# One late store of a cross-covariance attention kernel, cut into seven parts on two queues in place of four on one

## The chip, the cores and the metric

The kernel runs on one core of a Trainium2 chip. A core has five engines with instruction streams of their own: TensorE (PE), VectorE (DVE), ScalarE (ACT), GpSimd (POOL) and SyncE (SP). SP computes nothing; here it issues transfers. A transfer (DMA) moves data between the main memory (HBM) and the on-chip memory (SBUF, 128 partitions), and it is carried out by sixteen DMA engines that all queues share. A transfer is split over several of these engines; each moves its part in packets and closes it with a write of 4 bytes to a semaphore. The transfer has landed when all of those have come.

The metric is the time of one execution on the device in microseconds (us). The time before is the median of three runs, 128.60 us (128.47 to 128.75). The profile is of one more execution, of 128.35 us. Times within it are counted from its first instruction.

## The reference

Q, K and V are 8 x 12 x 512 x 64 (batch, heads, sequence, dim), in fp32. For each of the 96 heads:

```python
Q_norm = Q / (np.linalg.norm(Q, axis=-2, keepdims=True) + 1e-10)
K_norm = K / (np.linalg.norm(K, axis=-2, keepdims=True) + 1e-10)
attn = np.einsum('bhnd,bhne->bhde', Q_norm, K_norm)      # 64 x 64, over the sequence
attn = np.exp(attn - np.max(attn, axis=-1, keepdims=True))
attn = attn / (np.sum(attn, axis=-1, keepdims=True) + 1e-10)
out = np.einsum('bhnd,bhde->bhne', V, attn)
```

The inputs are 37.75 MB and the output 12.58 MB.

## The kernel before

**Tiling.** The heads are taken four at a time (a unit, 24 of them) and the units in pairs: twelve steps `s` = 0 to 11. A step loads its Q and K, casts them to bf16 (line 212), and forms the products Q'Q, Q'K and K'K of each head in one 128 x 128 Gram matrix on TensorE (line 232). The diagonal gives the norms, a quarter of the matrix the logits. Norms, exponentials and row sums follow on DVE, ACT and POOL (lines 239 to 290). V is loaded, cast (lines 168 and 170), transposed on TensorE (line 301) and multiplied with the attention matrix (line 318). The results are copied from PSUM into output tiles `so` (line 166 on ACT, line 168 on DVE) and stored.

**Stores.** A step has two output tiles, `so[s, 0]` and `so[s, 1]`, each filled by two copies; a tile is 128 partitions x 2 halves x 2 KB (512 KB), so that a store is 256 rows of 2 KB. Store 0 or 1 of step `s` goes out as one transfer (line 206), but for the store `FEW = (S - 3, 1)`, which is (9, 1), the sixth from the end: it leaves in four transfers, partitions 0 to 91, 92 to 99 and 100 to 127 of the first half (line 203) and all 128 of the second half (line 204). Two steps, and so four whole stores, follow it. There are thirteen `so` buffers.

**Order.** The program order of each engine is written by a planner (class `Order`): every piece of work has engines that may do it with a cost, pieces that it waits for, and a rank; pieces are placed one by one at the time at which the planner expects them to begin, and are then emitted in that order. Transfers are pieces of an engine called "DMA", and all but two early loads are issued on SP's queue, in the planner's order. `store` is called at its place in this order, whichever queue it issues on. The store (9, 1) is placed after the last piece of work of GpSimd, the scaling of K for step 11 (line 262).

**Waits.** A store waits for the two copies into its tile. Besides, SP's transfers take turns on eight semaphores, so that SP issues one only when the eighth before it has landed. The last thing that the program does is to wait until every transfer has landed, and then close.

Of the kernel before, what the change touches and what calls it, by code (L numbers as in the profile page):

```python
# [102 lines left out]
def kernel(  # L103
# [7 lines left out]
    nc = tc.nc  # L111
# [50 lines left out]
    qk32, v32, vb, qkb, gram, scr, kq, n2, r8, kqs, rq, lg, ex, ab, vps, vt, po, so = ({} for _ in range(18))  # L162
# [35 lines left out]
    def store(s, i):  # L198
        o = Of[s // 2, s % 2, i].rearrange("p r (j d) -> p r j d", d=D)
        if (s, i) == FEW:  # L200

            for a, b in ((0, 92), (92, 100), (100, 128)):
                nc.sync.dma_start(out=o[a:b, 0], in_=so[s, i][a:b, 0])
            nc.sync.dma_start(out=o[:, 1], in_=so[s, i][:, 1])
            return
        nc.sync.dma_start(out=o, in_=so[s, i])

# [139 lines left out]
    for i in range(NB["ab"]):  # L347
        a = const.tile([128, HU, 2 * D], BF16, name=f"ab{i}")
# [42 lines left out]
    for u in range(U):  # L391
        s, r = divmod(u, 2)
# [21 lines left out]
    for w in range(W):  # L414
        both = 2 * w >= BOTH
        for r in range(2):
            halves = (0, 1) if (w, r) == (W - 1, 1) else (None,)
            n = 2 * w + r - NB["v"]
# [22 lines left out]
    for s in range(S):  # L441
        for x in range(4):
            i, k = divmod(x, 2)
            n = 4 * s + x - 2
            wait = [("oc", n // 4, n % 4)] if n >= 0 else []
            order = [("ou", s, x - 1) if x else back("ou", s, 1, 3)]
            piece(("ou", s, x), {"PE": 0.5}, [("vc", s // 2, *t) for t in turns(s // 2) if t[0] // 2 == k] + [("nm", s)] + wait, order, R["ou"] + 0.01 * s, outs, s, x)
            n = 2 * s + i - NB["so"]
            free = [("st", n // 2, n % 2)] if k == 0 and n >= 0 else []
            order = [("oc", s, x - 1) if x else back("oc", s, 1, 3)]  # L450
            piece(("oc", s, x), {"ACT": 0.6, "DVE": (0.68, BIAS["oc"])} if s >= BOTH else {"ACT": 0.6}, [("ou", s, x)] + free, order, R["oc"] + 0.01 * s, ocopy, s, x)
        for i in range(2):
            order = [("st", s, 0) if i else back("st", s, 1, 1)]
            piece(("st", s, i), {"DMA": X}, [("oc", s, 2 * i), ("oc", s, 2 * i + 1)], order, v_at(2 * s + i) + ST_LAG, store, s, i)
# [43 lines left out]
```

## Time and profile before

| | |
|---|---|
| median of three runs | 128.60 us (128.47 to 128.75) |
| the profiled execution | 128.35 us |
| its span, first to last instruction | 126.5 us |
| busy: PE, DVE, ACT, POOL | 78.9, 90.7, 72.5, 37.4 us |
| moved over the span | 50.64 MB, 400 GB/s |
| SP's queue q1, share of the sixteen DMA engines' time | 96.5% |
| store (9, 1): its four issues on SP begin | 110.7 to 114.5 us |
| last compute instruction (ACT's copy into the last tile) ends | 115.6 us |

How to read it: a row of the second part of the page cuts the span into 40 slices of 3.16 us; a digit is the busy share in tenths, and GB/s is what all DMA engines moved together. A timeline line is start, length, engine, line, operation, output and input, and a count where like instructions are merged; an engine's name with a q (SPq) is its sequencer, which issues transfers. A table of windows gives for each stretch its length, each engine's busy time with the number of instructions, the clock granted to TensorE, the busy share of the DMA engines and GB/s. Packets of one engine overlap by some nanoseconds in the records, which is why that share can read 1.05 when all sixteen are full.

### The profile page before, as it was taken

Reading aid. Unit: us, or ns where it says so; the run is one execution under the profiler, and the core shown is the slowest. Engines: PE = TensorE matmul, PEld = TensorE weight load, DVE = VectorE, ACT = ScalarE, POOL = GpSimd, SP = SyncE. Lnnn points to the kernel's source line nnn. Section 1 sums busy time; section 2 is a strip of 40 time slices with the busy share of each in tenths; the row PEclk is TensorE's granted clock in tenths of the full one; section 3 lists DMA queues with packets and bytes.
Section 4 is the critical chain, followed back from the end, with each engine's and each line's share of the span. In section 5 each row is a group of like instructions: output and inputs, shape, how many; then the busy total and the mean of one; then the engine's idle time right before and its main releaser. Section 6 shows DMA issues by size and latency. Waiting matters only on the chain.

```text
span 126.5 us, 4885 instructions
## 1 busy us (share of the span) xinstructions
PE 78.9 (62%) x2128; PEld 64.2 (51%) x2128; DVE 90.7 (72%) x141; ACT 72.5 (57%) x220; POOL 37.4 (30%) x40
## 2 busy tenths in 40 slices
PE   0065393895964679958583999596676858473000
PEld 0054382784843568747372788484464746352000
DVE  3344749839899499899976798999999799740000
ACT  4000441539789077695883688694758969974000
POOL 4006307300745913043064303133363270300000
PEclk9999999999599555899998559959999999855555
DMA  3999999999999999999999999999999999999993
GB/s 129 408 434 411 427 413 421 413 434 408 430 417 418 409 422 417 398 414 425 422 417 412 418 419 421 416 423 423 401 415 411 402 401 407 400 407 408 405 382 149
DMA packets 15359, 50.64 MB, mean 400 GB/s; under 512 B 1130, under 2 KB 1130, under 8 KB 13930
## 3 DMA queue, kind: packets, MB, share of 16 engines
q1 hardware_dynamic: 15050, 49.29, 96.5%
q10 hardware_dynamic: 288, 1.05, 2.1%
q8 instruction: 16, 0.26, 0.7%
q14 instruction: 5, 0.04, 0.1%
HBM read 37.75 MB, written 12.58 MB: 398 GB/s over the span
## 4 chain that ended last, share of the span: by engine, by line
DVE 34%; DMA 21%; PE 19%; ACT 10%; issue 5%; POOL 2%; SPq 0%; DVEq 0%; ACTq 0%; POOLq 0%
DMA qk<-in_Q_dram 21%; DVE qkb L212 12%; PE gram L232 12%; DVE scr L239 7%; DVE ab L290 5%; ACT so L166 4%; PE po L318 3%; DVE vb L168 3%; ACT ex L281 3%; PE vps L301 3%; DVE n L251 3%; DVE vt L168 2%; ACT vt L166 2%; DVE so L168 1%; POOL kqs L262 1%
## 5 line engine op out<-in xcount | busy, mean ns | idle before, releaser
L232 PE MATMUL gram<-qkb 32*128 32x128 bf16 (+1 forms) x1504 | 36.9, 262 | 20.3 <-DVE qkb L212 7.1
L232 PEld LDWEIGHTS <-qkb 32*128 32x128 bf16 (+1 forms) x1504 | 31.0, 117 | 24.8 <-DVE qkb L212 8.9
L212 DVE CAST qkb<-qk 128x1024 bf16<-128x1024 f32 x48 | 35.3, 758 | 8.4 <-DMA qk<-in_Q_dram 6.8
L170 POOL TENSOR_SCALAR vb<-v 128x1024 bf16<-128x1024 f32 x19 | 22.0, 1169 | 43.9 <-DMA v<-in_V_dram 39.6
L166 ACT COPY so<-po 128x512 f32<-128x512 f32 x45 | 24.8, 593 | 6.6 <-PE po L318 6.5
L166 ACT COPY vt<-vps 128x1024 bf16<-128x1024 bf16 (+1 forms) x18 | 17.8, 987 | 16.5 <-PE vps L301 16.4
L318 PE MATMUL po<-ab,vt 128*64 128x128 bf16 x384 | 20.8, 252 | 5.1 <-ACT so L166 1.7
L301 PE MATMUL vps<-identb,vb 128*128 128x128 bf16 x192 | 18.4, 247 | 6.5 <-POOL vb L170 4.3
L262 POOL TENSOR_TENSOR kqs<-kq,r 64x512 f32<-64x512 f32 x12 | 14.1, 1171 | 26.7 <-ACT r L258 14.0
L239 DVE SCALAR_TENSOR_TENSOR scr<-gram,eye 64x512 f32<-64x512 f32 x24 | 16.5, 687 | 6.0 <-PE gram L232 5.8
L318 PEld LDWEIGHTS <-vt 128*64 128x64 bf16 x384 | 15.2, 127 | 9.4 <-issue 4.8
L301 PEld LDWEIGHTS <-vb 128*128 128x128 bf16 x192 | 13.5, 110 | 10.2 <-POOL vb L170 5.5
L281 ACT ACTIVATE ex<-lg,rq 128x64 f32<-128x64 f32 x48 | 14.5, 322 | 2.5 <-PE lg L275 2.3
L166 ACT COPY kq<-gram 64x512 f32<-64x512 f32 x12 | 7.0, 581 | 13.5 <-DVE scr L239 13.3
L290 DVE TENSOR_TENSOR ab<-ex,rinv 64x256 bf16<-64x256 f32 x24 | 13.4, 556 | 0.6
L281 ACT ACTIVATION_READ_ACCUMULATOR ex<-lg,rq 128x1 f32 x48 | 10.2, 213 | 0.0
L275 PE MATMUL lg<-eye,kqs 64*128 64x64 f32 x48 | 6.4, 258 | 4.3 <-POOL kqs L262 2.6
L251 DVE TENSOR_REDUCE n<-scr 128x8 f32<-128x512 f32 x12 | 8.1, 679 | 0.1
L168 DVE COPY vt<-vps 128x1024 bf16<-128x1024 bf16 (+1 forms) x8 | 7.9, 1020 | 0.1
L168 DVE CAST vb<-v 128x1024 bf16<-128x1024 f32 x5 | 7.0, 1399 | 1.3 <-DMA v<-in_V_dram 1.3
L275 PEld LDWEIGHTS lg<-eye,kqs 64*128 64x128 f32 x48 | 4.5, 156 | 6.1 <-POOL kqs L262 3.3
L287 DVE RECIPROCAL rinv<-esum 128x4 f32<-128x4 f32 x12 | 2.1, 172 | 3.4 <-ACT ex L281 3.2
(17 smaller groups left out, 16.0 us busy)
## 6 DMA issues: line engine op xcount, KB each, us to landing
out_dram<-so SPq DMA_DIRECT2D x23, 512.0 KB, 10.2
v<-in_V_dram SPq DMA_DIRECT2D x11, 1024.0 KB, 17.1
qk<-in_Q_dram SPq DMA_DIRECT2D x8, 1024.0 KB, 17.1
qk<-in_K_dram SPq DMA_DIRECT2D x8, 1024.0 KB, 17.9
qk<-in_Q_dram SPq DMA_DIRECT2D x8, 512.0 KB, 12.2
qk<-in_K_dram SPq DMA_DIRECT2D x6, 512.0 KB, 12.5
qk<-in_K_dram ACTq DMA_DIRECT2D x2, 512.0 KB
v<-in_V_dram SPq DMA_DIRECT2D x2, 512.0 KB
```

The lines of the kernel that those rows point to most:

```text
L166: nc.scalar.copy(o, i)
L168: nc.vector.tensor_copy(o, i)
L170: nc.gpsimd.tensor_scalar(out=o, in0=i, scalar1=1.0, scalar2=0.0, op0=ALU.mult, op1=ALU.add)
L212: nc.vector.tensor_copy(qkb[u][:, :, x * D:(x + 1) * D], qk32[s][:, x, r])
L232: nc.tensor.matmul(gram[s][:, h, r, 0], x, x, start=(t == 0), stop=(t == (T if u < WIDE else J) - 1))
L239: nc.vector.scalar_tensor_tensor(out=scr[s][half], in0=gram[s][half, :, :, 0, half].rearrange("p h r d -> p (h r) d"), scalar=1e-20, in1=e ...
L251: nc.vector.tensor_reduce(out=n2[s], in_=scr[s], axis=mybir.AxisListType.X, op=ALU.add)
L262: (nc.vector if eng == "DVE" else nc.gpsimd).tensor_tensor(out=kqs[s][HI], in0=kq[s][HI], in1=r8[s][HI, :, None].to_broadcast([D, 2 * HU, ...
L281: nc.scalar.activation(e[:, h, :], lg[s][:, h, :], AF.Exp, scale=rq[s][:, h:h + 1], accum_out=z[:, h:h + 1])
L290: nc.vector.tensor_tensor(out=a[half, :, half], in0=e[half], in1=ri[half, :, None].to_broadcast([D, HU, D]), op=ALU.mult,)
L301: nc.tensor.transpose(ps[:, c, n, :], vb[w][:, J * c + j].rearrange("p r d -> p (r d)"), identb)
L318: nc.tensor.matmul(po[s, x][e * D:(e + 1) * D, j].rearrange("p r d -> p (r d)"), v, ab[s][:, h, :])
```

## The change

In the store (9, 1) each half of the tile is cut anew. The first half goes in parts of 7, 37 and 84 partitions, the second in parts of 7, 31, 85 and 5. The first two parts of each half are issued by GpSimd, the others by SP. Bytes, tiles and all other transfers stay.

```diff
--- before.py
+++ after.py
@@ -199,9 +199,9 @@
         o = Of[s // 2, s % 2, i].rearrange("p r (j d) -> p r j d", d=D)
         if (s, i) == FEW:
 
-            for a, b in ((0, 92), (92, 100), (100, 128)):
-                nc.sync.dma_start(out=o[a:b, 0], in_=so[s, i][a:b, 0])
-            nc.sync.dma_start(out=o[:, 1], in_=so[s, i][:, 1])
+            for r, cuts in ((0, (7, 44, 128)), (1, (7, 38, 123, 128))):
+                for n, (a, b) in enumerate(zip((0,) + cuts, cuts)):
+                    (nc.gpsimd if n < 2 else nc.sync).dma_start(out=o[a:b, r], in_=so[s, i][a:b, r])
             return
         nc.sync.dma_start(out=o, in_=so[s, i])
 
```

## The prediction

> **What bounds the kernel now.** I read the page's slices first, then the tail in short windows, then SP's and GpSimd's timelines, then the single DMA packets.
>
> The page, slices of 3.16 us and the packet count:
>
> ```profile
> DMA  3999999999999999999999999999999999999993
> GB/s 129 408 434 411 427 413 421 413 434 408 430 417 418 409 422 417 398 414 425 422 417 412 418 419 421 416 423 423 401 415 411 402 401 407 400 407 408 405 382 149
> DMA packets 15359, 50.64 MB, mean 400 GB/s; under 512 B 1130, under 2 KB 1130, under 8 KB 13930
> ```
>
> The transfers are busy from the second slice to the last but one, while no compute engine is. The order of work decides little; how fast the sixteen DMA engines empty does. The tail by windows (from:to, length, busy time of PE, PEld, DVE, ACT, POOL, granted clock, DMA share, GB/s):
>
> ```profile
> 121.00:121.80 0.80, 0.00 (x0) 0.00 (x0) 0.00 (x0) 0.00 (x0) 0.00 (x0) 0.50 1.05 407
> 122.60:123.20 0.60, 0.00 (x0) 0.00 (x0) 0.00 (x0) 0.00 (x0) 0.00 (x0) 0.50 0.83 324
> 124.20:124.60 0.40, 0.00 (x0) 0.00 (x0) 0.00 (x0) 0.00 (x0) 0.00 (x0) 0.50 0.71 276
> 124.85:125.05 0.20, 0.00 (x0) 0.00 (x0) 0.00 (x0) 0.00 (x0) 0.00 (x0) 0.50 0.26 92
> 125.15:125.38 0.23, 0.00 (x0) 0.00 (x0) 0.00 (x0) 0.00 (x0) 0.00 (x0) 0.50 0.05 18
> 125.38:126.50 1.12, 0.00 (x0) 0.00 (x0) 0.00 (x0) 0.00 (x0) 0.00 (x0) 0.50 0.00 0
> ```
>
> Nothing computes here. At 407 GB/s sixteen engines work, 25.4 GB/s each, so a row of 2 KB takes 80 ns. The share falls in steps: about three engines have nothing left from 122.5, four are at work at 125, one alone after 125.15. The engines end unevenly, and the last sets the end. SP's and GpSimd's timelines:
>
> ```profile
> 104.25 5.75 SPq L206 DMA_DIRECT2D out_dram<-so  x5
> 110.66 2.84 SPq L203 DMA_DIRECT2D out_dram<-so  x3
> 114.49 0.37 SPq L204 DMA_DIRECT2D out_dram<-so  x1
> 115.81 4.22 SPq L206 DMA_DIRECT2D out_dram<-so  x4
> ```
>
> ```profile
> 107.64 1.04 POOL L262 TENSOR_TENSOR kqs<-kq,r 64x512 f32<-64x512 f32 x1 [3.76 <-ACT r L258]
> ```
>
> SP issues the changed store at 110.66 to 114.86 and four whole stores behind it. GpSimd has nothing to do after 108.68.
>
> **Which engine ends when.** The packet records have start, duration, bytes and queue, but no engine. They can be strung together: in the tail a 2 KB packet starts 80 ns after the one before it on its engine, and a 4-byte completion write closes each engine's part of a DMA. Between those writes the rows can be counted, which shows who took what of the 92, 8, 28 and 128 partitions: four engines (A) took 23+1+2+8 = 34 rows, four (B) 1+2+8 = 11, six (C) 2+8 = 10, two (D) 8. So 92 went to 4 engines, 8 to 8, 28 to 14, 128 to 16: each time the largest number up to 16 that divides the partitions, in sets that contain each other. The page agrees: 69 DMAs of 16 completion writes and 4+8+14 make its 1130 small packets. Last completion write of each engine, us of the span:
>
> ```
> A (34 rows)  124.10  124.54  124.91  125.38
> B (11 rows)  122.27  124.00  124.88  124.99
> C (10 rows)  122.36  124.80  124.91  124.99  125.00  125.14
> D (8 rows)   122.46  125.03
> ```
>
> (Where two engines ran in step their chains can be exchanged; the classes hold.) The last, 125.38, is one of A. Behind it lie 1.15 us of landing and closing to the span's 126.53, and 1.8 us outside the span to this execution's 128.35 us; the median of the runs is 128.60, 0.25 more, and I carry differences over to it. If all ended together the end would come 1.0 us earlier (the mean of the sixteen distances to 125.38): the most that any shifting of rows can gain.
>
> **The change part by part.** *SP's side.* Three DMAs go in place of four. By the pattern above 84 partitions go to 14 engines, 6 rows each, 85 to five, 17 each, and 5 to the same five, 1 each. An issue takes 0.29 to 0.37 us and one goes away; worth nothing, since SP spends this stretch waiting for old stores to land and a store lands 6.0 us (median after 108) after its issue. SP keeps eight transfers open, so the four stores behind may issue one place (1.3 us) earlier; also nothing while every engine's queue is full, which the share of 1.05 up to 122 shows.
>
> *GpSimd's side.* Four DMAs are added to its queue. They wait for ACT's two copies into this tile, which end at 109.43 (the ninth and tenth from the last), and nothing stands behind them there. No row shows a DMA issued by GpSimd; from below it is SP's 0.29 us, from above GpSimd's slowest compute instruction near the end, 1.1 us. I take 1.1: all four are out by 114. They would matter only if the 37 rows started after 122.4 (37 x 0.08 = 3.0 before 125.38), so 8 us of cover lie between. At the closing SP waits for four more transfers; its waits there take about 0.03 us each, 0.1 at most, none taken.
>
> *Rows per engine.* This is the whole change, and its unknown is where GpSimd's pieces land. From SP's pattern 7 goes to seven engines, 37 and 31 (prime) to one each. As to which, I suppose that they are dealt out to consecutive engines: 7 to A and three of B, 37 to the fourth of B, 7 to C and one of D, 31 to the other of D, once round. Then, new rows less old ones: each A 1+6+17+1 = 25, less 34, -9; the fifth engine of the 85 (in B) 25-11 = +14; two of B 7-11 = -4; one of B 37+6-11 = +32; C 7-10 = -3; one of D 1-8 = -7, the other 31-8 = +23. The sum is 0. If the +32 and +23 fall on the early ones of B and D, and the +14 on B's second, the new ends are:
>
> A: 125.38 - 0.72 = 124.66. B: 122.27 + 2.56 = 124.83, 124.00 + 1.12 = 125.12, 124.99 - 0.32 = 124.67. C: 125.14 - 0.24 = 124.90. D: 122.46 + 1.84 = 124.30, 125.03 - 0.56 = 124.47.
>
> The last is then 125.12, a gain of 0.26 us; if the +14 did not bind, C at 124.90, a gain of 0.48. I take 0.3, since an execution nearer the median has a later end to trim: 128.6 - 0.3 = 128.3. Bounds of the unknown place: best 0.48 gained; worst, 37 rows on B's latest, 124.99 + 2.56 = 127.55, 2.2 lost.
>
> The Trainium skill, page "DMA: Bandwidth & Descriptors", section "Why a DMA increments its semaphore by 16 and not by 1", says that SP's pieces use the lowest-numbered engines and GpSimd's consecutive ones from a round-robin cursor; by it, from a cursor at 0, 37 rows go to engine 7 and 31 to engine 15, as I supposed. No row of this trace shows that. The same page, section "Latency and other measured facts", speaks against the change: engines 7 and 15 are usually slower than the rest, with a cause that it calls a guess. If they were the late ones of B and D here, the sum would be 2.2 us slower, 130.8; the trace shows that one of B and one of D are early by 3 us, and not which.
>
> **The rivals.** *The long pieces land on a late engine* (slower). Mechanism: GpSimd's 37 or 31 rows, or the fifth part of the 85, go to an engine of its class with no lead. A late B has room for 0.4/0.08 = 5 rows before it becomes the last. Prices: only the +14 wrong, 124.99 + 1.12 = 126.11, +0.73, 129.3; only the +23 wrong, 125.03 + 1.84 = 126.87, +1.5, 130.1; the +32 wrong, +2.2, 130.8. For it: the records do not number engines inside a class. Against it: each of the three has an engine in its class whose lead (3.1, 2.9, 1.4 us) exceeds what is added (2.56, 1.84, 1.12).
>
> *GpSimd spreads each piece over all sixteen* (37 as three rows on twelve and one, 31 as two on fifteen and one, 7 as one on seven). Then A gets -3, the fifth +20, C at most +1: A 125.14, C 125.22, the fifth 125.60 if it is B's second: +0.2, 128.8; up to +1.2 if it is a late one. For it: GpSimd's queue need not divide as SP's does. Against: nothing in the trace. (The skill's section on the semaphore's 16 reports such spreading for some copies of GpSimd's.)
>
> *No change that shows*: the closing or the DMA engines' stalls (some packets take up to 0.23 us for 0.084) give back the 0.3: 128.6. The three runs of before spread by 0.28 us, as much as the gain.
>
> **How the numbers follow.** Long pieces and the fifth part on engines with lead: 0.55, of which 0.07 turns out within 0.2%. On late ones: 0.25. Spread over sixteen: 0.12, half of it within 0.2%. No change that shows: 0.08. A measurement of this kernel tells about 0.2%, 0.26 us, from no change. Faster: 0.48. Same: 0.07 + 0.06 + 0.08 = 0.21. Slower: 0.25 + 0.06 = 0.31. Range: below, the gain of 0.48 and 0.2 of scatter, 127.9; above, it takes in the fifth part misplaced (129.3) with scatter, 129.6, and leaves out the misplaced 31 and 37 (0.13). The likeliest case's own range is 127.9 to 128.5.
>
> **What would show it.** In the packets: SP's pieces on 14, 5 and 5 engines; on GpSimd's queue 82 rows, 37 and 31 of them on one engine each. In the tail's windows: a share near 1.05 up to about 124 and a steeper fall. On GpSimd: four issues soon after 109.4. Wrong if an engine works alone for 0.5 us or more at the end, if the 37 rows are spread, or if the early engines are others in this kernel.

## The result

The changed kernel takes 128.64 us (median of 20 runs, 128.51 to 129.13); the kernel before, on the same chip, 128.46 us (128.32 to 128.75). The ratio is 1.0015, with a 95% interval of 1.0008 to 1.0022: 0.19 us slower, less than the 0.2% that the prediction called telling, but with an interval that excludes no change. The forecast was 128.3, 0.3 us faster; the time lies inside its range of 127.9 to 129.6, on the other side of no change. The profiled execution of the changed kernel took 128.58 us, with a span of 126.8; that of before 128.35 and 126.5.

The page of the changed kernel, its packet count and its queues (packets, MB, share of the sixteen engines):

```profile
DMA packets 15403, 50.64 MB, mean 399 GB/s; under 512 B 1201, under 2 KB 1201, under 8 KB 13974
q1 hardware_dynamic: 14950, 49.12, 96.0%
q0 software_dynamic: 144, 0.17, 0.4%
```

A queue q0 is new: GpSimd's, with 144 packets for 82 rows. Its issues and SP's, in the timeline of the changed kernel:

```profile
107.83 1.04 POOL L262 TENSOR_TENSOR kqs<-kq,r 64x512 f32<-64x512 f32 x1 [3.75 <-ACT r L258]
109.92 2.25 POOL L204 DMA_DIRECT2D out_dram<-so  x4 [1.05 <-ACT so L166]
```

```profile
110.85 2.79 SPq L204 DMA_DIRECT2D out_dram<-so  x3
114.77 4.59 SPq L206 DMA_DIRECT2D out_dram<-so  x4
```

GpSimd waits for ACT's copy, as foreseen, and has issued all four by 112.2; its pieces land about 5 us later. SP needs three issues. No compute engine has another order of work. The tail of the changed kernel in the windows that the prediction showed for before:

```profile
121.00:121.80 0.80, 0.00 (x0) 0.00 (x0) 0.00 (x0) 0.00 (x0) 0.00 (x0) 0.50 1.06 410
122.60:123.20 0.60, 0.00 (x0) 0.00 (x0) 0.00 (x0) 0.00 (x0) 0.00 (x0) 0.50 0.84 324
124.20:124.60 0.40, 0.00 (x0) 0.00 (x0) 0.00 (x0) 0.00 (x0) 0.00 (x0) 0.50 0.75 292
124.85:125.05 0.20, 0.00 (x0) 0.00 (x0) 0.00 (x0) 0.00 (x0) 0.00 (x0) 0.50 0.50 195
125.15:125.38 0.23, 0.00 (x0) 0.00 (x0) 0.00 (x0) 0.00 (x0) 0.00 (x0) 0.50 0.22 80
125.38:126.50 1.12, 0.00 (x0) 0.00 (x0) 0.00 (x0) 0.00 (x0) 0.00 (x0) 0.50 0.01 4
```

The gap that the change was to fill is still there: 324 GB/s between 122.6 and 123.2, as before, so three engines have run out by 122.5 again. What is different is the very end, where about eight engines (195 GB/s) work at 125 instead of four, and three (80) instead of one after 125.15. The last packet ends at 125.49 us, against 125.39.

**Where the rows went.** The packets of q0 say how the pieces were split without any chain. The piece of 37 partitions is 12 packets of 4 KB, 12 of 2 KB and one of 2 KB joined with its completion write: three rows on each of twelve engines and one on a thirteenth. The piece of 31 is 15 packets of 4 KB and one of 2 KB: two rows on fifteen engines, one on the sixteenth. Each 7 is seven packets of 2 KB. The 37 and 31 rows are not on one engine each. Strung together as in the prediction, the engines end as follows (us of the span):

```
                        before                                     changed
A                       124.10 124.54 124.91 125.38 (34 rows)      124.13 124.37 124.71 125.30 125.49 (31 rows)
  with the fifth
B and C, without it     122.27 122.36 124.80 124.88 124.91         122.20 122.47 125.05 125.06 125.19 125.23
  (in before all ten)   124.99 124.99 125.00 125.14, 124.00        125.24 125.25 125.49
D                       122.46 125.03                              122.01 124.73
```

Three engines are out by 122.5 again: none was given the work meant for it. With the pieces split in this way from the first engine on, each of A has 31 rows in place of 34, and one engine of B 31 in place of 11. The five with 31 rows can't be told apart in this trace; that the one which ended at 124.00 before is now among the last (125.30 or 125.49) is inferred from its rows.

**What the end is made of.** The records of the semaphores, from the last landing to the end of the span, give the rest. Parts of the span in us:

```
                         before   changed
first data packet at      1.75     1.85
from it to last packet  123.63   123.64
to the last landing       0.31     0.36
closing, to the end       0.83     0.96
```

The transfers take as long as before. The first packet comes 0.10 later in this one execution (in the other kernels below it comes at 1.74 to 1.77, and nothing in the change stands ahead of it; left open). The closing is 0.13 longer; only one execution of each kernel was profiled, but the parts of these 0.13 come back in the other kernels below. Line 493 is the end of the program; first the rows of before, then those of the changed kernel (durations in ns, shortest/median/longest):

```profile
L493 SPq EVENT_SEMAPHORE  x7: 17/28/28, 120.6 to 126.5; - x7
L493 POOLq DRAIN  x3: 34/78/1146, 107.6 to 126.3; - x3
L493 POOLq EVENT_SEMAPHORE_RANGE_CLEAR  x1: 96/96/96, 126.1 to 126.1; - x1
```

```profile
L493 SPq EVENT_SEMAPHORE  x9: 17/28/28, 120.7 to 126.7; - x9
L493 POOLq DRAIN  x3: 34/102/5561, 111.2 to 126.5; - x3
L493 POOLq EVENT_SEMAPHORE_RANGE_CLEAR  x1: 139/139/139, 126.4 to 126.4; - x1
```

SP waits for the transfers' semaphores one after the other, in a fixed order. In before the last store is on the one that it waits for last: that wait is met at 125.717, 0.017 after the last landing, and no other follows. With three SP transfers in place of four the last store is on the one before: its wait is met at 125.863, again 0.017 after the landing, and one more follows at 125.925, 0.062 later. (The two waits that GpSimd's transfers add stand ahead of these and are met before the landing.) GpSimd's drain (102 ns, not 78) and its clearing of the semaphores (139, not 96) add 0.024 and 0.043. Together 0.129 us.

### The profile page after: what moved, and what is told of

Read it like the earlier page. It is cut to its first block, busy times and chain, and to the rows that moved or that the text cites. A ratio compares the mean times of both kernels' runs of the same rounds, so it can differ in the third digit from the quotient of the medians.

```text
span 126.8 us, 4890 instructions
## 1 busy us (share of the span) xinstructions
PE 76.7 (61%) x2128; PEld 62.4 (49%) x2128; DVE 92.8 (73%) x141; ACT 72.5 (57%) x220; POOL 38.7 (31%) x44
## 4 chain that ended last, share of the span: by engine, by line
DVE 39%; DMA 21%; PE 13%; ACT 12%; issue 4%; POOL 1%; DVEq 0%; SPq 0%; ACTq 0%; POOLq 0%
DMA qk<-in_Q_dram 21%; DVE qkb L212 16%; DVE scr L239 7%; PE gram L232 7%; DVE ab L290 6%; ACT vt L166 4%; DVE vb L168 4%; PE vps L301 3%; ACT ex L281 3%; ACT so L166 3%; DVE vt L168 2%; PE po L318 2%; DVE n L251 2%; ACT kq L166 1%; DVE so L168 1%
## 5 line engine op out<-in xcount | busy, mean ns | idle before, releaser
L212 DVE CAST qkb<-qk 128x1024 bf16<-128x1024 f32 x48 | 36.3, 781 | 8.7 <-DMA qk<-in_Q_dram 7.0
L170 POOL TENSOR_SCALAR vb<-v 128x1024 bf16<-128x1024 f32 x19 | 21.1, 1120 | 46.0 <-DMA v<-in_V_dram 45.8
L318 PE MATMUL po<-ab,vt 128*64 128x128 bf16 x384 | 19.2, 237 | 6.4 <-DVE ab L290 2.5
L318 PEld LDWEIGHTS <-vt 128*64 128x64 bf16 x384 | 13.7, 117 | 10.5 <-issue 4.4
L168 DVE CAST vb<-v 128x1024 bf16<-128x1024 f32 x5 | 7.7, 1537 | 1.2 <-DMA v<-in_V_dram 1.1
```

Of the source, the lines that this page charges most:

```text
L168: nc.vector.tensor_copy(o, i)
L170: nc.gpsimd.tensor_scalar(out=o, in0=i, scalar1=1.0, scalar2=0.0, op0=ALU.mult, op1=ALU.add)
L212: nc.vector.tensor_copy(qkb[u][:, :, x * D:(x + 1) * D], qk32[s][:, x, r])
L318: nc.tensor.matmul(po[s, x][e * D:(e + 1) * D, j].rearrange("p r d -> p (r d)"), v, ab[s][:, h, :])
```

## The experiments

All change only the parts in which the store (9, 1) leaves, against the kernel before. The first diff is whole; where a later one shows a single line, it stands in place of the line `for q, r, a, b in` of the first: queue, half, and the partitions from and to. Where a time is given without a ratio, it is that of a single execution.

**One piece on GpSimd's queue.**

```diff
-            for a, b in ((0, 92), (92, 100), (100, 128)):
-                nc.sync.dma_start(out=o[a:b, 0], in_=so[s, i][a:b, 0])
-            nc.sync.dma_start(out=o[:, 1], in_=so[s, i][:, 1])
+            for q, r, a, b in ((nc.sync, 0, 0, 92), (nc.gpsimd, 0, 92, 100), (nc.sync, 0, 100, 128), (nc.sync, 1, 0, 128)):
+                q.dma_start(out=o[a:b, r], in_=so[s, i][a:b, r])
```

> The four parts of before (92, 8, 28, 128), but the 8 partitions are issued by GpSimd. Seven of GpSimd's partitions went to seven engines in the changed kernel, so 8 go to eight, as on SP: no engine gets another number of rows. Theory (spread and closing): GpSimd's long pieces were spread over the sixteen engines, so the change moved hardly any rows to the engines with lead, and its loss is a fixed price at the closing once GpSimd's queue is used at all, 0.13 us between the last landing and the end: ratio 1.0010 (1.0005 to 1.0015). Rival (rows): GpSimd's queue is free and the change lost by putting more rows on late engines: ratio 1.000.

Measured: 1.0006 (0.9996 to 1.0017). Strung together, its packets put the 8 rows on the four engines of A and the four of B, as they do from SP (chains in step can be exchanged there), and the ends are those of before (A's last and the last packet at 125.39). Closing 0.95 us in place of 0.83. The trace shows the price of the theory; the ratio is compatible with it and with none.

**Three pieces on GpSimd's queue.**

```diff
+            for q, r, a, b in ((nc.sync, 0, 0, 92), (nc.gpsimd, 0, 92, 100), (nc.gpsimd, 0, 100, 128), (nc.gpsimd, 1, 0, 128)):
```

> The parts of before, but 8, 28 and 128 are issued by GpSimd and only 92 by SP. Spread as even pieces of up to ceil(n/16) rows they give each engine the rows that it had (1 on eight, 2 on fourteen, 8 on sixteen). Theory (spread and closing): the same price as with one piece, about 0.13 us, ratio 1.0010 (1.0005 to 1.0016), since the closing is paid once. Rival (price by transfer): each GpSimd transfer costs, so three cost three times what one costs. Rival (rows): ratio 1.000.

Measured: 1.0015 (1.0007 to 1.0024), last packet at 125.32, closing 1.09. So not the same price as one piece. But it is no price of a transfer on GpSimd either: behind the last landing stand three more waits of SP's in place of one, since SP issues only one part here and the last store has moved three semaphores back. That led to the theory of turns, tried in the sixth and seventh experiments.

**The store whole.**

```diff
-            for a, b in ((0, 92), (92, 100), (100, 128)):
-                nc.sync.dma_start(out=o[a:b, 0], in_=so[s, i][a:b, 0])
-            nc.sync.dma_start(out=o[:, 1], in_=so[s, i][:, 1])
+            nc.sync.dma_start(out=o, in_=so[s, i])
```

> The store goes out as one transfer, 16 rows on each engine. Rows theory, 80 ns a row against the ends in the trace of before: A -18 rows; B +5, 124.99 + 0.40 = 125.39; C +6, 125.14 + 0.48 = 125.62; D +8, 125.03 + 0.64 = 125.67, so the end is 0.29 us later, ratio 1.0022 (1.001 to 1.003). If single engines' rows did not set the end: 1.000.

Measured: 1.0036 (1.0024 to 1.0048), 0.46 us. The last packet ends at 125.73, where 125.67 was worked out from rows of 80 ns. All sixteen now have equal rows, so the packets no longer tell the classes apart; but eight engines end at 122.6 to 124.2, where 80 ns a row puts the four of A (18 rows less), the three with lead and the one of B that ended at 124.00 (122.7 to 124.4). In the window near the end six to seven engines are at work on average:

```profile
125.15:125.60 0.45, 0.00 (x0) 0.00 (x0) 0.00 (x0) 0.00 (x0) 0.00 (x0) 0.50 0.42 164
```

The sum was short by the closing, 1.04 us in place of 0.83. Rows on single engines do set the end.

**The changed kernel's rows by SP alone.**

```diff
+            for q, r, a, b in ((nc.sync, 0, 0, 84), (nc.sync, 0, 84, 128), (nc.sync, 1, 0, 85), (nc.sync, 1, 85, 90), (nc.sync, 1, 90, 118), (nc.sync, 1, 118, 128)):
```

> Nearly the rows per engine that the changed kernel has if GpSimd spreads its pieces (31 on the first five, 13 to 8 on the next nine, 2 and 1 on the last two), by SP alone, in six transfers (84, 44; 85, 5, 28, 10: 31 on the first five, 13 on five, 12, 8 on three, 0 on two). Theory (spread and closing): the transfers end as in the changed kernel, but the closing is that of before: 0.18 - 0.13 = 0.05 us slower than before, ratio 1.0004 (0.9995 to 1.001). Rival (rows): the whole loss stays, 1.0015.

Measured: 1.0019 (1.0010 to 1.0029). The closing is not that of before but 1.02 us, again by the turn, and the last packet ends at 125.64, on the first five engines; the fifth engine's sum was 124.00 + 20 x 0.08 = 125.60. It doesn't separate the two theories as it was meant to, for a second reason too: no engine ends before 124.8, so the three with lead have lost it. Probably they ran dry while SP's six small transfers held six of the eight places that it keeps open; no run shows that alone.

**Marks, first try.**

```diff
+            for q, r, a, b in ((nc.sync, 0, 0, 119), (nc.sync, 0, 119, 128), (nc.sync, 1, 0, 120), (nc.sync, 1, 120, 128)):
```

> SP alone, in four transfers of 119, 9, 120 and 8 partitions: 17 rows on seven engines, 1 on nine, 8 on fifteen, 1 on eight, so that the eighth engine has 10 rows, the ninth 9, the sixteenth 0, and each of the three can be told from the rest in the packets. Prediction's supposition: the early engine of B is the eighth and that of D the sixteenth; then the chain with 10 rows ends near 122.2 us and the one with 0 near 121.8. Rival: the eighth or the sixteenth is a late engine and ends near 124.9 or 124.4. Rows theory: two of the fifth to seventh engine are late ones with 16 rows more, 124.99 + 1.28 = 126.27, so the end is 0.9 us later, 129.4.

Measured: 129.26 us, last packet at 126.27, as worked out. Which chain is the eighth engine's can't be told: with so few rows some engines run dry for 0.2 to 0.4 us, and the chains break there. Inconclusive on the question it was made for.

**The changed kernel with SP's turn restored.**

```diff
+            for q, r, a, b in ((nc.gpsimd, 0, 0, 7), (nc.gpsimd, 0, 7, 44), (nc.sync, 0, 44, 86), (nc.sync, 0, 86, 128), (nc.gpsimd, 1, 0, 7), (nc.gpsimd, 1, 7, 38), (nc.sync, 1, 38, 123), (nc.sync, 1, 123, 128)):
```

> The changed kernel, but SP's 84 goes as 42 and 42 (3 rows on fourteen engines, twice): the same rows on every engine, and one SP transfer more, so that the last store is again on the semaphore that the closing waits for last. Theory (closing in turns): one wait of 0.06 us less behind the last landing than in the changed kernel, closing 0.90 in place of 0.96 us, ratio to before 1.0010 (1.0003 to 1.0017). Rival (GpSimd's queue has one price, whatever the turn): closing 0.96, ratio 1.0015.

Measured: closing 0.901, as the theory of turns has it; 0.067 over before's is the price of GpSimd's queue itself. The time did not follow: 1.0019 (1.0005 to 1.0032). In its profile the last packet ends at 125.61, on one of the five engines with 31 rows, so a later tail hides the 0.06. The interval is too wide to say more.

**The even store in four transfers.**

```diff
+            for q, r, a, b in ((nc.sync, 0, 0, 64), (nc.sync, 0, 64, 128), (nc.sync, 1, 0, 64), (nc.sync, 1, 64, 128)):
```

> 16 rows on each engine, as with the whole store, but in four transfers of 64 partitions (4 rows on sixteen engines, four times), so that the last store is on the semaphore that the closing waits for last. Theory (closing in turns): three waits less than with the whole store, closing 0.84 in place of 1.04 us, ratio 1.0036 - 0.0015 = 1.0021 (1.0012 to 1.0030). Rival (closing is noise): closing 1.04, ratio 1.0036.

Measured: closing 0.844, three waits less than with the whole store, and 1.0010 (1.0000 to 1.0020) against 1.0036 (1.0024 to 1.0048). The rows are the same on every engine; the two intervals do not meet. So the four transfers are the better ones, and the shorter closing, 0.19 us, is on that side. It is not all that differs: the ratios are 0.33 us apart, the medians with their own before 0.19, the store was also cut in four, the two ran on different chips, and in the one profiled execution (129.02, the slowest of its runs) the last packet ends at 126.06, 0.33 later than with the whole store.

**The seven parts on SP.**

```diff
+            for q, r, a, b in ((nc.sync, 0, 0, 7), (nc.sync, 0, 7, 44), (nc.sync, 0, 44, 128), (nc.sync, 1, 0, 7), (nc.sync, 1, 7, 38), (nc.sync, 1, 38, 123), (nc.sync, 1, 123, 128)):
```

> The seven parts of the changed kernel, all on SP, which gives a prime number of partitions to one engine: the first engine gets 1+37+6+1+31+17+1 = 94 rows, 60 more than before. Rows theory: it becomes the last at its end in before (124.1 to 125.4) plus 60 x 0.08 = 4.8 us, so the end is 3.5 to 4.8 us later, 132.0 to 133.4. Rival (a transfer's parts even out, or the long piece hides under other engines' work): under 1 us later.

Measured: 132.33 us. The windows of its end:

```profile
125.00:126.20 1.20, 0.00 (x0) 0.00 (x0) 0.00 (x0) 0.00 (x0) 0.00 (x0) 0.50 0.86 333
126.20:129.10 2.90, 0.00 (x0) 0.00 (x0) 0.00 (x0) 0.00 (x0) 0.00 (x0) 0.50 0.07 25
```

One engine alone, at 25 GB/s, for 2.9 us: this is what a long piece on one engine without lead looks like, and what the prediction expected of GpSimd's pieces in its rival. It ends at 129.15, 3.8 us after before. Besides, the others stand still for a while. SP's timeline, what SP waited for at line 203 from 112 us on (us in total, times, longest), and the GB/s of the queues between 108 and 127 us in slices of 0.49 us:

```profile
110.80 7.93 SPq L203 DMA_DIRECT2D out_dram<-so  x7
119.84 2.95 SPq L205 DMA_DIRECT2D out_dram<-so  x4
```

```profile
SPq L203 <- DMA out_dram<-so: 5.9, 6, 1.1
```

```profile
GB/s 440 384 384 392 401 410 405 405 401 414 405 410 405 401 410 410 401 410 349 319 298 310 319 319 173 43 65 397 388 414 410 414 401 401 405 405 410 332 30 26
```

The seven small parts take seven of SP's eight places, and for six of them SP first waits until an old store has landed. The four whole stores behind them are issued only from 119.84 to 122.8. The rate falls from 117 on, is at 43 and 65 GB/s between 120.2 and 121.2, and is back at 400 once the first of them moves: until then, it seems, most engines have nothing queued.

**Marks that leave the rows alone.**

```diff
+            for q, r, a, b in ((nc.sync, 0, 0, 92), (nc.sync, 0, 92, 99), (nc.sync, 0, 99, 114), (nc.sync, 0, 114, 128), (nc.sync, 1, 0, 128)):
```

> SP alone, 92, 7, 15, 14 and 128 partitions: the rows of before but for one or two (34 on four engines, 11 on the next three, 10 on seven, 9, 8), so every engine should end where it did in before within 0.1 to 0.2 us; but the parts of 7 and of 15 tell the eighth engine from the fifth to seventh and the sixteenth from the fifteenth. Prediction's supposition: the fifth to seventh end near 124.0, 124.9 and 125.0, none early; the eighth is the early one among the other seven, beside the early one of C (two of seven near 122.2); the sixteenth is early (122.4), the fifteenth late (125.0). Rival: one of the fifth to seventh is near 122.3, or the fifteenth is early.

```diff
+            for q, r, a, b in ((nc.sync, 0, 0, 92), (nc.sync, 0, 92, 95), (nc.sync, 0, 95, 100), (nc.sync, 0, 100, 128), (nc.sync, 1, 0, 128)):
```

> SP alone, 92, 3, 5, 28 and 128 partitions: again the rows of before but for one, and the parts of 3 and 5 tell the fourth engine from the first three and the fifth from the rest. Prediction's supposition: the fifth engine is the one of B that ends near 124.0 (12 to 13 rows of room). Rival: it ends near 124.9, and then has room for 5 rows at most, or it is the early one. Open: which of A's four is the last, 125.4.

Measured: 128.59 and 128.56 us, and clean chains. With the parts of 7 and 15: the fifth to seventh engine end at 123.98, 125.02 and 125.19, none early; the next seven at 123.49, 123.53 and from 125.07 to 125.52; the fifteenth at 125.37, the sixteenth at 123.63. With 3 and 5: the fifth ends at 124.08, the fourth at 124.96, and the last of A, 125.51, is one of the first three. Since one of B is early and it is not the fifth, sixth or seventh, it is the eighth. So the eighth and the sixteenth lead and the fifth has room, as the prediction supposed. (With five SP transfers the three leads before the last engine shrink from 2.9 to 3.1 us to 1.9 to 2.4, and the closing is 0.95.)

**Fewer rows on A.**

```diff
+            for q, r, a, b in ((nc.sync, 0, 0, 76), (nc.sync, 0, 76, 100), (nc.sync, 0, 100, 128), (nc.sync, 1, 0, 128)):
```

> SP alone and four transfers as in before, but 76, 24, 28 and 128: A gets 31 rows in place of 34, the next eight 12, two 10, two 8. Rows theory with the ends of before: A 125.38 - 0.24 = 125.14, C's latest at most 125.14 + 0.16 = 125.30 (if it is one of the four with 12; 125.14 if not), B 124.99 + 0.08 = 125.07; the end 0.08 to 0.24 us earlier, closing unchanged, ratio 0.9982 to 0.9994. Rival (the executions' own scatter of the ends is as large): 1.000.

```diff
+            for q, r, a, b in ((nc.sync, 0, 0, 76), (nc.sync, 0, 76, 84), (nc.sync, 0, 84, 128), (nc.sync, 1, 0, 128)):
```

> SP alone, four transfers: 76, 8, 44 and 128, which gives 32 rows to the first four engines, 13 to the next four, 12 to three, 8 to five. With the ends of the clean traces (before, the two with one or three pieces on GpSimd, the two with marks), moved by 80 ns a row, the last engine ends 0.16 us earlier on average; closing as in before: ratio 0.9987 (0.998 to 0.9995). Rival (the ends scatter from one execution to the next by as much as is gained): 1.000.

Measured: 0.9992 (0.9983 to 1.0001), twice. Medians of 128.37 and 128.36 us against 128.47 and 128.41. Neither is told from before by its interval. In the profiled execution of the second A's last ends at 125.39 in spite of two rows less; in that of the first, which is the slowest of its runs (128.94), all of A ends 0.6 to 0.7 us later than in before. From one execution to the next A's ends move by more than three rows are worth.

## Why the prediction was wrong

**The bound** was right: the DMA engines' unevenness at the end, the price of a row (80 ns, found in the whole store, in the first marks and in the 25 GB/s of the one engine that works alone in the seven parts on SP), and the class ends, which come back within 0.1 to 0.2 us in most traces.

**Which engines lead** was right, though the trace of before could not number them: eighth, sixteenth and fifth, as the marks show.

**The step that failed** is "37 and 31 (prime) to one each", taken over from SP's pattern. That pattern holds for SP alone (with the seven parts on SP the first engine got both long pieces). GpSimd's queue cut n partitions here into ceil(n/16) rows an engine: 37 into three rows on each of twelve engines and one on a thirteenth, 31 into two on each of fifteen and one on the sixteenth. The prediction had named that as a sign of being wrong. By the strung chains these pieces begin at the first engine each time: the 8 of the first experiment lay on the first eight, and in the changed kernel engines of A have rows of both pieces of 7. (This placing is less sure than the split, since chains in step can be exchanged; for the pieces of 7 it is worth one row.) Placed so, the eighth engine, which was to get 32 rows more, kept its 11, and the sixteenth, which was to get 23 more, lost seven. This was the prediction's second rival, to which it gave 0.12. Its rows were right (31 on the first five engines) and its time nearly (128.8 for a start of 128.6, +0.2; measured +0.19), but not for its reason alone: the fifth engine, put at 125.60, is among five whose last ended at 125.49 here, 125.61 and 125.64 in the two other kernels that give it 31 rows, while in this profile the transfers together took only 0.01 longer. The sum of that rival has no closing in it, which is most of what the profile shows; that its time came out so near is partly luck.

The page "DMA: Bandwidth & Descriptors" of the Trainium skill, section "Why a DMA increments its semaphore by 16 and not by 1", names both: consecutive engines from a cursor as the rule, and ceil(partitions/16) as an exception measured for some copies. All of GpSimd's pieces here (7, 8, 28, 31, 37, 128) fit the exception, and 37 and 31 contradict the rule. Its section "Latency and other measured facts", by which engines 7 and 15 are usually the slower ones, did not hold in the kernels with marks: there the eighth and the sixteenth, which are 7 and 15 if SP's pieces lie on the lowest-numbered engines, are two of the three that finish first. The page ties its guess at the cause to GpSimd's queue, and the marks use SP's alone.

**The closing** was put at "0.1 at most, none taken", from SP's waits of 0.03 us each; that is the length of one wait's record (28 ns), while from one wait to the next it takes 0.06. In the profile the closing costs 0.129: 0.067 for GpSimd's queue and 0.062 because one SP transfer less moves the last store off the semaphore that is waited for last. The step "one goes away; worth nothing" counted SP's issue and its queue, and missed that the number of SP's transfers decides the order in which the program's last waits are met. By the profile the closing is two thirds of the measured 0.19 us. The runs' times do not show it by itself: GpSimd's queue with one piece is compatible with no loss (1.0006), and the changed kernel with the turn restored, whose closing is 0.062 shorter, was not faster (1.0019). The remaining 0.06 is not settled either: in the profile the first packet comes 0.10 later and the last landing about 0.04 longer after the last packet, and the runs' medians can't resolve it.

**Right besides**: GpSimd's issues (0.51 to 0.70 us each, put at 1.1) hide completely; SP's fewer issues do not matter in the stream; no compute moves.

The two versions of SP alone with less on A look 0.1 us faster than before, but neither is proven; the share of the possible 1.0 us that lies on the eighth and the sixteenth engine can't be reached with sets that always begin at the first engine. Whether rows on these two would have brought the gain that was forecast is therefore not shown.

## What to carry to other kernels

Where the DMA engines are full to the end, count rows per engine and look which one ends last: moving rows is worth 80 ns each here, on that engine alone. Before a queue is used to aim at an engine, see on a trace how that queue splits a piece; SP's and GpSimd's queues split the same number of partitions differently. And look behind the last landing: the waits that close the program are met in a fixed order, so by these traces the number of transfers moves the end by 0.06 us a turn without touching the stream.

## What was not expected of the hardware

- GpSimd's queue joined the rows of neighbouring partitions into packets of 4 KB (0.159 us for one), where SP's queue sent two of 2 KB (0.084 each); and it wrote far more small packets than there were engines with data: 25 of 4 bytes with the first piece of 7 rows, so that 82 rows made 144 packets, 55 with data and 89 of 4 or 8 bytes.
- The closing took 0.834 to 0.844 us with four SP parts and none on GpSimd, 0.948 and 0.950 with five, 1.037 with one, 1.020 with six, 1.083 with seven; with GpSimd's queue in use 0.901 (four SP parts), 0.948 and 0.963 (three), 1.091 (one).
- Three engines are early by some 2 to 3 us in most of these kernels; where marks name them, they are the eighth, the sixteenth and one of the ninth to fourteenth. Why was not tried, and the records do not tell whether they are faster or had less to move.
